# A short-convolution mixer: the planner's order of VectorE, ScalarE, GpSimd and SyncE replaced by a table

## The chip, the cores and the metric

The kernel runs on one core of one Trainium2 chip. The metric is the time of one execution in microseconds of the device. Before the change the median of three runs is 757.72 us (756.49 to 759.22).

## The reference

The model has one layer, a gated short convolution between two RMS norms; everything is float32, 1024 positions by 1024 features.

```python
u = rms_norm(x, pre_norm)                      # (1024, 1024)
z, bg, cg, v = split(u @ w_in, 4, axis=-1)     # w_in (1024, 8192), four of 2048
y = bg * causal_dwconv(cg * v, conv_w) * silu(z)   # three taps along the positions
m = y @ w_out                                  # w_out (2048, 1024)
out = x + rms_norm(m, post_norm)
```

## The kernel before, in words

**The matrix products.** TensorE multiplies fp32r. To keep float32 accuracy each operand is split into a high half (rounded to fp32r) and a low half (the rest), and each product is three matmuls: low by high, high by low, high by high. Both matrix products are computed in 2x2 blocks with seven products, called a, b, c, e, d, f, g, in place of eight. The weights of a product are then a block or a sum of blocks. For b, f and g a second level of the same kind lies inside, with 256 wide products; its weights have names that begin with d.

**The names.** A name in the profile is that of the tile:

- raw is a 256 KB block of w_in that SyncE's queue has loaded; se, sc and sf are sums of blocks, dsb, dsf and dsg those of the second level. They are made by GpSimd (`add_s`, L791; `deep_sums`, L1439).
- wah, wch, weh, wdh and dwb1h, dwf1h and so on are high halves, copied by ScalarE; wal, wcl, wel, wdl, dwb1l, dwf1l, dwf2l are the low halves, subtracted by VectorE (`split`, L809; `split_low`, L840; `deep_prep`, L1454). For some of them ScalarE also copies the source into a PSUM bank, beside, from which VectorE reads (`split_by_bank`, L833).
- u_a to u_g are the stationary operands made of u. The place of u_g is lent out in the middle of the kernel, and `restore_u` (L1723) loads the source (ug) again and splits it, the low half on VectorE.
- px, pv, px2b, pv2b, py2b, px2f, pv2f are PSUM banks. Their contents are taken over into sna, snc and sne (ScalarE copies, VectorE adds), then cv holds the convolution on VectorE and s the gated result, which SyncE's queue stores.
- tb, t and t23 are sums of w_out for the second product. ry and ru are pages with its operands, oy and ou those operands split in halves (`split_pages`, L1620); po_x is its bank.
- acc holds a row tile of the result, xr the residual, gpost the post-norm's weights, ve_post the mean square and rs_post its inverse root, which GpSimd makes (`finish`, L1951).

**The loops.** The first product runs over chunks of 128 channels, two pairs of blocks for each (an even and an odd number, such as wcl_28 and wcl_29), with the second-level products between them; a new round of dwb, dwf and dwg comes with every chunk. From about 604 us the second product follows, in units a, c, e, d, g over four row tiles, with small ones between. Each engine runs its own instructions in the order in which they stand in its queue and waits at the head of it for what is missing.

**What sets the order.** The program writes its operations in the order of the algorithm, and from `plan.record()` (L1780) to `plan.flush(PLAN)` (L2107) they are only recorded: 6577 operations, 4038 of them matmuls, 940 for VectorE, 392 for GpSimd, 794 for ScalarE and 412 for SyncE. `call` (L290) notes what each needs, `link` (L354) ties them, `deadlines` (L375) works out from modelled durations when each has to be done for TensorE not to wait, with a table that shifts the due times of single operations (`PLAN["boost"]`). `arrange` (L428) then runs a model of the engines in time: the due operation next for each engine, one lock between VectorE and GpSimd, and a free page out of 32 for each tile (`home`, L645). Where VectorE has nothing to do it takes an addition from GpSimd (`take`). TensorE's order is that of the program throughout. `emit` (L658) issues what came out. Since all recorded operations are issued from one line, they all have L292 in the profile before. The start of the kernel, to about 48 us, and the work behind the last matmuls (`finish_last`) are issued without a plan.

Of the kernel before, what the change touches and what calls it, by code (L numbers as in the profile page):

```python
# [27 lines left out]
PLAN = {  # L28
    "end": 14.0,
    "psum": 3.0,  # L30
    "store": 6.0,
    "turns": 1,
    "apart": 11.0,
    "hard": 2.0,
    "lock": 0.3,
    "sum": 10.0,
    "early": 0.0,
    "gap": 0.5,
    "least": 1.0,
    "free": 40.0,  # L40
    "take": 11.0,
    "held": {"snc_1": 1.95},
    "ahead": {"sync": 24.0, "gpsimd": 18.0, "scalar": 11.0, "vector": 11.0},
    "busy": {"vector": 1.9, "scalar": 0.3, "gpsimd": -2.1},
    "slack": {"tensor": 1.0, "gpsimd": 0.8, "sync": 1.0, "scalar": 0.1, "vector": 0.1},
    "boost": {
# [38 lines left out]
    },  # L85
}
# [123 lines left out]
U_SLOTS = (5, 4, 2, 6, 1, 3, 0, 0, 5, 2, 6, 4, 1, 3, 0, 5, 2, 6, 4, 1, 6, 3, 0, 4, 2, 5, 6, 1, 0, 3, 2, 4, 5, 6, 0, 4, 1, 5, 3, 6, 0, 2)  # L210
# [8 lines left out]
class Shelves:  # L219

    def __init__(self, ctx, tc):
        self.at, self.slots = {}, list(U_SLOTS)
        for n, (slots, room) in enumerate(U_LAYOUT):
            pool = ctx.enter_context(tc.tile_pool(name=f"up{n}", bufs=1))
            self.at.update({s: pool for s in slots})
            if n == 0:
                self.low = ctx.enter_context(tc.tile_pool(name="low_pages", bufs=1))
            gap(ctx, tc, f"room{n}", room)

    def tile(self, shape, dtype, tag, **kw):  # L230
        s = self.slots.pop(0)
        return self.at[s].tile(shape, dtype, tag=f"u{s}", **dict(kw, bufs=1))
# [21 lines left out]
class Plan:  # L254
# [120 lines left out]
    def deadlines(self, p):  # L375

        ops = self.ops
        limit = {}
        for op in ops:
            op.est = 0.0  # L380
        for turn in range(p["turns"]):
            for op in reversed(ops):
                if op.engine == "tensor":
                    op.late = op.ideal
                    continue
                late = op.pos + p["end"]
                for o in op.feeds:
                    f = ops[o]
                    late = min(late, f.late - op.lat - (p["hard"] if f.engine == "tensor" else 0.0) - (p["lock"] if op.lock else 0.0))
                for t in op.tiles:  # L390
                    if t in limit and all(x.key != t.key for x in op.news):
                        late = min(late, limit[t] - op.lat)
                if any(t.summed for t in op.tiles):
                    late = min(late, max(op.ideal, op.est) + p["psum"])
                if op.engine == "sync" and any(isinstance(a, View) and a.tile.space == "sbuf" for a in op.args[1:]):
                    late = min(late, max(op.ideal, op.est) + p["store"])
                if op.tiles and not op.news and all(t.space == "dram" for t in op.tiles):
                    late = min(late, max(op.ideal, op.pos) + p["sum"])
                op.late = late
            for op in ops:  # L400
                if op.engine != "tensor":
                    op.late = max([ops[o].late + 0.01 for o in op.needs], default=op.late) if op.needs and max(ops[o].late for o in op.needs) >= op.late else op.late
                op.est = max([ops[o].est + ops[o].lat for o in op.needs] + [op.late - p["ahead"].get(op.engine, 10.0) if op.news else 0.0, 0.0])
                if op.engine == "tensor":
                    op.est = op.ideal
# [22 lines left out]
    def arrange(self, p):  # L428
# [4 lines left out]
        for n, by in p.get("boost", {}).items():  # L433
            ops[n].late -= by
# [1699 lines left out]
```

## Time and profile before

| what | value |
|---|---|
| median of 3 runs | 757.72 us (756.49 to 759.22) |
| profiled execution, its own time | 758.85 us |
| its span in the trace | 757.1 us |
| granted TensorE clock | 0.998 |
| idle PE between 300 and 740 us | 2.69 us |
| waits of weight loads, 300 to 750 us | 6.1 us in 11 |

PE is TensorE's matmuls, PEld its weight loads, DVE is VectorE, ACT ScalarE, POOL GpSimd and SP SyncE. The matmuls are pipelined, so their ends are modelled, and the spans of GpSimd are rough. A row of a timeline has start, length, engine, line, operation and the output and inputs by the names above, without their numbers. In square brackets stands the idle time of the engine just before, with what ended it. In a view of waits a row names who waited, what for, the sum in us, how many times and the longest.

### The profile page before, as it was taken

To read this page: it belongs to the slowest core of one execution; us is meant where nothing else is said; L and a number is where in the kernel's file an instruction comes from. 1 tells how busy PE (TensorE), PEld (TensorE's weight loads), DVE (VectorE), ACT (ScalarE), POOL (GpSimd) and SP (SyncE) were. 2 spreads that over 40 slices of the span, in tenths; PEclk is the share of its full clock that TensorE was granted. 3 is DMA by queue.
4 is the path that set the end of the run, shared out by engine and by line. 5 is a ranking of instruction groups with operands and counts; after the bars stand their busy time and mean duration, and the time that the engine had idled before them with its cause. 6 is when DMAs were issued, how large, how long until landed. Compare 5 with 4: busy or idle time off the path is not lost.

```text
span 757.1 us, 12810 instructions
## 1 busy us (share of the span) xinstructions
PE 745.2 (98%) x4320; PEld 660.0 (87%) x4320; DVE 677.9 (90%) x1022; ACT 458.7 (61%) x880; POOL 462.4 (61%) x416
## 2 busy tenths in 40 slices
PE   8999999999999999999999999999999999999996
PEld 7888889999999999989998988899888889889885
DVE  6899988999998988999999999898999999877994
ACT  7765588675656564655556565666553666565831
POOL 2509997889686777697788777685739100600421
PEclk9999999999999999999999999999999999999999
DMA  9313325244333548476949383928465999566842
GB/s 313 78 49 91 111 77 162 102 142 133 98 119 98 177 115 224 111 193 163 264 119 273 95 239 80 270 95 217 118 183 179 339 362 309 201 226 206 283 149 111
DMA packets 117137, 130.11 MB, mean 172 GB/s; under 512 B 7320, under 2 KB 74704, under 8 KB 116944
## 3 DMA queue, kind: packets, MB, share of 16 engines
q1 hardware_dynamic: 112560, 120.77, 50.1%
q0 software_dynamic: 4352, 8.39, 7.2%
q8 instruction: 34, 0.56, 0.3%
q14 instruction: 31, 0.25, 0.1%
q10 hardware_dynamic: 160, 0.14, 0.1%
HBM read 101.74 MB, written 44.30 MB: 193 GB/s over the span
## 4 chain that ended last, share of the span: by engine, by line
PE 75%; DVE 8%; POOL 6%; issue 4%; DMA 3%; ACT 3%; SPq 0%; POOLq 0%; DVEq 0%; ACTq 0%
PE px L292 29%; PE pv L292 12%; PE po_x L292 8%; PE px2b L292 4%; PE po_v L292 3%; PE pp L292 3%; PE px2f L292 3%; PE px2g L292 2%; PE pv2f L292 2%; PE pv2b L292 2%; PE pb_x L292 1%; POOL dsb L292 1%; DMA raw<-in_sc_w_in 1%; PE py L292 1%; PE py2b L292 1%
## 5 line engine op out<-in xcount | busy, mean ns | idle before, releaser
L292 PE MATMUL px<-u_a,wah 128*128 128x512 f32 x248 | 75.1, 383 | 0.0
L292 PE MATMUL px<-u_c,wch 128*128 128x512 f32 x248 | 74.9, 382 | 0.0
L292 PE MATMUL px<-u_d,wdh 128*128 128x512 f32 x248 | 74.9, 382 | 0.0
L292 PE MATMUL pv<-u_e,weh 128*128 128x512 f32 x248 | 74.7, 381 | 0.0
L292 ACT COPY beside<-raw 128x512 f32<-128x512 f32 x67 | 39.6, 591 | 34.2 <-DVE dwf2l L292 9.9
L292 PEld LDWEIGHTS px<-u_a,wah 128*128 128x128 f32 x248 | 46.5, 188 | 8.0
L292 PEld LDWEIGHTS px<-u_c,wch 128*128 128x128 f32 x248 | 46.5, 188 | 7.9
L292 PEld LDWEIGHTS pv<-u_e,weh 128*128 128x128 f32 x248 | 46.5, 188 | 7.7
L292 PEld LDWEIGHTS px<-u_d,wdh 128*128 128x128 f32 x248 | 46.5, 188 | 7.6
L292 DVE SCALAR_TENSOR_TENSOR cv<-gpad,cw,cv 128x1024 f32<-128x1024 f32 x32 | 49.8, 1557 | 3.3 <-ACT cv L292 3.2
L292 POOL TENSOR_TENSOR sf<-raw,sc 128x512 f32<-128x512 f32 x30 | 44.5, 1484 | 7.1 <-DVE sc L292 5.5
L292 PE MATMUL px<-u_c,wcl 128*128 128x512 f32 x124 | 47.9, 386 | 0.2 <-DVE wcl L292 0.2
L292 PE MATMUL px<-u_a,wal 128*128 128x512 f32 x124 | 47.8, 385 | 0.0
L292 PE MATMUL px<-u_d,wdl 128*128 128x512 f32 x124 | 47.7, 385 | 0.0
L292 PE MATMUL pv<-u_e,wel 128*128 128x512 f32 x124 | 47.5, 383 | 0.0
L292 POOL TENSOR_TENSOR sc<-se,raw 128x512 f32<-128x512 f32 x25 | 35.9, 1434 | 19.0 <-DVE se L292 10.4
L292 POOL TENSOR_TENSOR rs_post<-ve_post,minus_half 128x1 f32<-128x1 f32 x7 | 6.5, 941 | 65.9 <-DVE ve_post L292 65.9
L292 POOL TENSOR_TENSOR raw<-raw,raw 128x512 f32<-128x512 f32 x31 | 43.5, 1403 | 4.2 <-DVE se L292 3.8
L292 POOL TENSOR_TENSOR se<-raw,raw 128x512 f32<-128x512 f32 x22 | 32.2, 1463 | 18.7 <-DMA raw<-in_sc_w_in 9.4
L292 ACT COPY sna<-px 128x512 f32<-128x512 f32 x30 | 17.6, 585 | 34.4 <-PE px L292 34.4
L292 DVE TENSOR_TENSOR wcl<-sc,wch 128x512 fp32r<-128x512 f32 x31 | 33.8, 1089 | 5.0 <-ACT wch L292 5.0
L292 DVE TENSOR_TENSOR wel<-se,weh 128x512 fp32r<-128x512 f32 x31 | 32.3, 1043 | 0.0
(486 smaller groups left out, 2615.8 us busy)
## 6 DMA issues: line engine op xcount, KB each, us to landing
raw<-in_sc_w_in SPq DMA_DIRECT2D x128, 256.0 KB, 5.2
y_d<-cv SPq DMA_DIRECT2D x16, 512.0 KB, 2.7
s_d<-s SPq DMA_DIRECT2D x32, 256.0 KB, 4.9
t_d<-in_sc_w_out POOLq DMA_DIRECT2D x16, 512.0 KB, 8.5
tb<-in_sc_w_out SPq DMA_DIRECT2D x16, 256.0 KB, 3.5
t_d<-in_sc_w_out SPq DMA_DIRECT2D x16, 256.0 KB, 4.9
t_d<-t_d SPq DMA_DIRECT2D x16, 256.0 KB, 4.6
s<-y_d SPq DMA_DIRECT2D x16, 256.0 KB, 4.6
```

What stands on the lines that cost most here:

```text
L292: getattr(engine, name)(*(self.plain(a) for a in args), **{k: self.plain(a) for k, a in kw.items()})
```

## The change

The planner goes, with its costs, its shifted due times and its choice of pages. In its place stand three tables. `ORDER` lists the operations by their number, and a negative number stands for so many matmuls; `HOMES` gives the page of each tile as it comes up; `BY_VECTOR` names 48 additions that the program writes for GpSimd and that VectorE makes. `arrange` only reads the tables. `U_SLOTS`, the places of the u operands, is looked up by name and no longer by turn.

```diff
-PLAN = {
-    "end": 14.0,
-    "psum": 3.0,
...
-    "boost": {
-        0: -1.88, 1: 31.37, 2: -1.93, 4: 16.59, 5: 18.27, 6: 0.14, 20: 0.84, 21: 1.2, 22: 10.67, 27: -0.09,
...
-}
+ORDER = (
+    350, 0, 1, -4, 5, 60, -2, 203, 22, -3, 2, -3, 6, 20, 21, -2, 24, -3, 246, -3, 7, 4, 25, 41, -2, 3, 247, -2, 23, -5, 42, -1, 91,
...
+)
+
+HOMES = (
+    15, 16, 21, 22, 24, 29, 31, 19, 20, 1, 15, 27, 16, 14, 18, 26, 12, 2, 22, 20, 21, 16, 3, 24, 26, 27, 1, 31, 17, 19, 30, 23, 22,
...
+)
+
+BY_VECTOR = (
...
+    2671, 2672, 2674, 2810, 2867, 2868, 3028, 3147, 3399, 3593, 3948, 4110, 4248, 4464, 4605, 4606, 4662, 4840, 5780, 5782, 5783,
+    6354, 6363, 6432, 6445,
+)
...
-U_SLOTS = (5, 4, 2, 6, 1, 3, 0, 0, 5, 2, 6, 4, 1, 3, 0, 5, 2, 6, 4, 1, 6, 3, 0, 4, 2, 5, 6, 1, 0, 3, 2, 4, 5, 6, 0, 4, 1, 5, 3, 6, 0, 2)
+U_SLOTS = {
+    "u_a": 5, "u_b": 4, "u_c": 2, "u_e": 6, "u_d": 1, "u_f": 3, "xb": 0, "u_g": 0, "ou_a0": 5, "oy_a0": 2,
...
-        s = self.slots.pop(0)
+        s = U_SLOTS[kw["name"]]
...
-    def deadlines(self, p):
...
-    def flush(self, p):
         self.link()
-        order = self.arrange(p)
-        self.emit(order)
-
-    def arrange(self, p):
...
+        self.emit(self.arrange())
+
+    def arrange(self):
+
+        ops, order, homes = self.ops, [], iter(HOMES)
+        matmuls = iter([op for op in ops if op.engine == "tensor"])
+        for n in ORDER:
+            order += [next(matmuls) for _ in range(-n)] if n < 0 else [ops[n]]
+        for n in BY_VECTOR:
+            ops[n].engine, ops[n].name = "vector", (self.nc.vector, ops[n].name[1])
+        for op in order:
+            for x in sorted(op.news, key=lambda x: x.n):
+                if x.key[1] == "pg":
+                    x.slot = next(homes)
+        self.slots = list(homes)
+        assert len(order) == len(ops)
         return order
...
-    def home(x, slots):
...
-            plan.flush(PLAN)
+            plan.flush()
```

What is computed, the matmuls, their order and the operations themselves stay. VectorE gets 954 of the recorded operations (940 before), GpSimd 378 (392 before): net, 17 additions go from GpSimd to VectorE (thirteen before the last stage; four are acc<-acc,xr of the last stage) and 3 from VectorE to GpSimd. Up to about 48 us, and behind the last matmul, each engine's order is the same as before. The recorded operations now have L449. The number at the end of a name in the rows below counts tiles, and it is not the same number before and after; the number ahead of it is that of the block, the chunk or the row tile.

**The first place: VectorE at about 543 to 550 us**, where u_g is restored and wcl_29 made. cv is the convolution, s0 and s4 the gated sums, sna, sne and snc what was taken over from the banks. Before:

```order
L292 TENSOR_TENSOR cv_13_6384<-cv_13_6384,sna_27_6067 128x512
L292 TENSOR_TENSOR sne_28_6426<-px_28_6278,sne_28_6426 128x512
L292 SCALAR_TENSOR_TENSOR s0_13_6365<-s1_13_6276,s0_13_6365 128x512
L292 TENSOR_TENSOR u_g_584<-ug_6346,u_g_584 128x2x256
L292 SCALAR_TENSOR_TENSOR s4_13_6522<-cv_13_6384,s0_13_6365 128x512
L292 TENSOR_TENSOR snc_28_6396<-px2f_14_6461,snc_28_6396 128x256
L292 TENSOR_TENSOR wcl_29_6537<-sc_29_6391,wch_29_6441 128x512
```

After:

```order
L449 TENSOR_TENSOR u_g_584<-ug_6294,u_g_584 128x2x256
L449 TENSOR_TENSOR sne_28_6438<-px_28_6289,sne_28_6438 128x512
L449 TENSOR_TENSOR cv_13_6392<-cv_13_6392,sna_27_6066 128x512
L449 SCALAR_TENSOR_TENSOR s0_13_6300<-s1_13_6262,s0_13_6300 128x512
L449 TENSOR_TENSOR wcl_29_6511<-sc_29_6397,wch_29_6446 128x512
L449 SCALAR_TENSOR_TENSOR s4_13_6534<-cv_13_6392,s0_13_6300 128x512
L449 TENSOR_TENSOR snc_28_6402<-px2f_14_6463,snc_28_6402 128x256
```

u_g went ahead of the cv product with sna_27, of sne_28 and of s0_13; wcl_29 went ahead of s4_13 and snc_28.

**The second place: VectorE and GpSimd at about 325 to 331 us**, where dwf1l_8 (a low half of the second level) and its source dsf0_8 are made. VectorE before:

```order
L292 TENSOR_TENSOR sne_16_3784<-px_16_3640,sne_16_3784 128x512
L292 TENSOR_TENSOR snc_16_3751<-px2f_8_3814,snc_16_3751 128x256
L292 TENSOR_TENSOR wel_17_3872<-se_17_3714,weh_17_3826 128x512
L292 TENSOR_TENSOR snc_16_3751<-pv_16_3748,snc_16_3751 128x512
L292 TENSOR_TENSOR sna_16_3671<-px2b_8_3774,sna_16_3671 128x256
L292 TENSOR_TENSOR sna_17_3867<-pv2b_8_3875,sna_17_3867 128x256
L292 TENSOR_TENSOR dwf1l_8_3907<-dsf0_8_3816,dwf1h_8_3898 128x512
```

VectorE after:

```order
L449 TENSOR_TENSOR sne_16_3775<-px_16_3643,sne_16_3775 128x512
L449 TENSOR_TENSOR dwf1l_8_3875<-dsf0_8_3810,dwf1h_8_3834 128x512
L449 TENSOR_TENSOR sna_16_3670<-px2b_8_3772,sna_16_3670 128x256
L449 TENSOR_TENSOR snc_16_3756<-px2f_8_3825,snc_16_3756 128x256
L449 TENSOR_TENSOR snc_16_3756<-pv_16_3750,snc_16_3756 128x512
L449 TENSOR_TENSOR sna_17_3863<-pv2b_8_3880,sna_17_3863 128x256
L449 TENSOR_TENSOR wel_17_3914<-se_17_3707,weh_17_3865 128x512
```

dwf1l_8 went ahead of the step of sna_16, both of snc_16, that of sna_17 and of wel_17; wel_17 went from the third place to the last. GpSimd before, from the first half of dsf0_8 to its second:

```order
L292 TENSOR_TENSOR t23_13_3808<-tb1_13_3703,tb0_13_3697 128x256
L292 TENSOR_TENSOR dsf0_8_3816<-sf_17_3755 128x256
L292 TENSOR_TENSOR t23_13_3808<-t23_13_3808,tb0_13_3697 128x256
L292 TENSOR_TENSOR tb1_13_3703<-tb1_13_3703,t23_13_3808 128x256
L292 TENSOR_TENSOR dsb1_8_3852<-raw_16_01_3459,raw_17_01_3664 128x256
L292 TENSOR_TENSOR dsb1_8_3852<-raw_16_01_3459,dsb0_8_3745 128x256
L292 TENSOR_TENSOR dsf0_8_3816<-dsf0_8_3816,sf_16_3668 128x256
```

GpSimd after:

```order
L449 TENSOR_TENSOR dsf0_8_3810<-sf_17_3767 128x256
L449 TENSOR_TENSOR t23_13_3808<-t23_13_3808,tb0_13_3648 128x256
L449 TENSOR_TENSOR dsf0_8_3810<-dsf0_8_3810,sf_16_3650 128x256
L449 TENSOR_TENSOR tb1_13_3806<-tb1_13_3806,t23_13_3808 128x256
L449 TENSOR_TENSOR dsb1_8_3856<-raw_16_01_3454,raw_17_01_3613 128x256
L449 TENSOR_TENSOR dsb1_8_3856<-raw_16_01_3454,dsb0_8_3736 128x256
```

The second half of dsf0_8 went ahead of the tb1 step and of both halves of dsb1_8, and the first t23_13 step isn't GpSimd's any more.

**The third place: the last stage, about 710 to 724 us.** GpSimd before, the inverse roots and the additions of the residual:

```order
L292 TENSOR_TENSOR rs_post0_8335<-ve_post0_8328,minus_half_90 128x1
L292 TENSOR_TENSOR rs_post1_8337<-ve_post1_8330,minus_half_90 128x1
L292 TENSOR_TENSOR acc_7302<-acc_7302,xr01_7923 128x512
L292 TENSOR_TENSOR acc_7302<-acc_7302,xr11_8033 128x512
L292 TENSOR_TENSOR rs_post2_8411<-ve_post2_8388,minus_half_90 128x1
L292 TENSOR_TENSOR rs_post3_8413<-ve_post3_8391,minus_half_90 128x1
L292 TENSOR_TENSOR acc_7302<-acc_7302,xr21_8254 128x512
L292 TENSOR_TENSOR acc_7302<-acc_7302,xr31_8274 128x512
```

VectorE after, the same additions among the steps on acc and the splits of oy_d and ou_g:

```order
L449 SCALAR_TENSOR_TENSOR acc_7385<-acc_7385,rs_post0_8320,gpost1_7233 128x512
L449 TENSOR_SCALAR ve_post1_8352<-so_7664 128x1
L449 SCALAR_TENSOR_TENSOR acc_7385<-acc_7385,rs_post0_8320,xr00_8018 128x512
L449 TENSOR_TENSOR acc_7385<-acc_7385,xr01_7734 128x512
L449 SCALAR_TENSOR_TENSOR acc_7385<-acc_7385,rs_post1_8359,xr10_8016 128x512
L449 TENSOR_TENSOR oy_d1_8247<-ry_d13_8096,oy_d1_8247 128x512
L449 TENSOR_SCALAR ve_post3_8386<-so_7664 128x1
L449 SCALAR_TENSOR_TENSOR acc_7385<-acc_7385,rs_post1_8359,gpost1_7233 128x512
L449 TENSOR_TENSOR acc_7385<-acc_7385,xr11_8020 128x512
L449 TENSOR_TENSOR ou_g0_8344<-ru_g01_8213,ou_g0_8344 128x512
```

The additions of xr01 and xr11 stand on VectorE between the scaled steps on acc; those of xr21 and xr31 follow further down, and GpSimd keeps the roots alone.

More of the change, by code (lines that the diff above doesn't have):

```diff
@@ L1 @@
-import heapq
 from contextlib import ExitStack
@@ L27 @@
 )
-PLAN = {
-    "end": 14.0,
-    "psum": 3.0,
[L31 to L45, printed above, removed]
-    "boost": {
[38 rows of a table removed]
-    },
-}
+ORDER = (
[164 rows of a table added]
+)
+HOMES = (
[35 rows of a table added]
+)
+BY_VECTOR = (
+    1, 201, 249, 286, 333, 351, 353, 745, 895, 1012, 1039, 1096, 1390, 1391, 1448, 1451, 1598, 1743, 1800, 1807, 1958, 2153, 2307,
+    2671, 2672, 2674, 2810, 2867, 2868, 3028, 3147, 3399, 3593, 3948, 4110, 4248, 4464, 4605, 4606, 4662, 4840, 5780, 5782, 5783,
+    6354, 6363, 6432, 6445,
+)
 BY_BANK_DEEP = (("b", 0), ("b", 1), ("b", 2), ("f", 0), ("f", 2))
@@ L209 @@
 LOW_PAGES = (3, 10, 11, 13, 15, 16, 5, 6, 8, 9)
-U_SLOTS = (5, 4, 2, 6, 1, 3, 0, 0, 5, 2, 6, 4, 1, 3, 0, 5, 2, 6, 4, 1, 6, 3, 0, 4, 2, 5, 6, 1, 0, 3, 2, 4, 5, 6, 0, 4, 1, 5, 3, 6, 0, 2)
+U_SLOTS = {
+    "u_a": 5, "u_b": 4, "u_c": 2, "u_e": 6, "u_d": 1, "u_f": 3, "xb": 0, "u_g": 0, "ou_a0": 5, "oy_a0": 2,
[4 rows of a table added]
+}
 def gap(ctx, tc, name, size):
@@ L221, in __init__ @@
     def __init__(self, ctx, tc):
-        self.at, self.slots = {}, list(U_SLOTS)
+        self.at = {}
         for n, (slots, room) in enumerate(U_LAYOUT):
@@ L373, in link @@
                 self.users.setdefault(t, []).append(op)
-    def deadlines(self, p):
[L377 to L405, printed above, removed]
-            allocs, tiles = {}, {}
-            for op in ops:
-                for t in op.news:
-                    allocs.setdefault(t.key, []).append(op.late)
-            for t, users in self.users.items():
-                if t.space != "dram":
-                    tiles.setdefault(t.key, []).append((max(u.est + u.lat for u in users), t.n, t))
-            for key, ts in tiles.items():
-                at = sorted(allocs.get(key, []))
-                spare = self.spare(key)
-                for k, (end, _, t) in enumerate(sorted(ts, key=lambda x: x[:2])):
-                    if k + spare < len(at):
-                        limit[t] = max(at[k + spare] - p["gap"], end + p["least"])
@@ L644, in home, with flush @@
-    @staticmethod
-    def home(x, slots):
-        name = x.kw["name"]
-        low, high = ([s for s in slots if (s in LOW_PAGES) == side] for side in (True, False))
-        if name[:2] in ("wb", "wf", "wg"):
-            first = low
-        elif name[0] == "w" or name[:2] == "dw":
-            first = high
-        else:
-            first = slots
-        s = (first or slots)[0]
-        slots.remove(s)
-        return s
+    def flush(self):
+        self.link()
+        self.emit(self.arrange())
```

203 lines of the change are left out of this document (removed), and 238 rows, old and new, of tables (HOMES, ORDER, PLAN, U_SLOTS).

## The prediction

> **What bounds the kernel now.** The measure of "no change" is 0.3%, some 2.3 us. The profiled execution took 758.85 us: a span of 757.1 us and 1.75 us around it. It lies 1.13 us above the median of 757.72, so the sum is made against 758.85, and 1.13 is taken off at the end. I read the page's busy line first.
>
> ```profile
> PE 745.2 (98%) x4320; PEld 660.0 (87%) x4320; DVE 677.9 (90%) x1022; ACT 458.7 (61%) x880; POOL 462.4 (61%) x416
> ```
>
> TensorE comes first, VectorE follows at 90%. Whether that is one regime or several is told by the table of stretches. The columns are start and end, length, and then busy time (with instructions) of PE, PEld, DVE, ACT and POOL, granted clock, DMA share and GB/s.
>
> ```profile
> 48.00:300.00 252.00, 252.00 (x1468) 224.88 (x1468) 230.91 (x337) 163.54 (x322) 203.55 (x181) 1.00 0.42 124
> 300.00:340.00 40.00, 39.61 (x246) 35.56 (x245) 36.68 (x56) 22.95 (x45) 30.74 (x28) 1.00 0.63 161
> 340.00:440.00 100.00, 99.27 (x610) 89.01 (x609) 93.81 (x137) 58.54 (x112) 78.86 (x72) 1.00 0.70 188
> 440.00:560.00 120.00, 118.49 (x731) 106.35 (x730) 111.37 (x172) 72.24 (x139) 78.59 (x72) 1.00 0.65 172
> 560.00:740.00 180.00, 179.94 (x993) 157.35 (x992) 161.56 (x251) 103.29 (x200) 53.27 (x41) 1.00 0.72 242
> ```
>
> The clock is full throughout, and the order of the matmuls isn't touched, so all that a new order of the other engines can win is time in which TensorE stands still. From 48 to 300 us there is none. From 300 to 740 PE is idle for 0.39+0.73+1.51+0.06 = 2.69 us. VectorE has 252-230.91, 3.32, 6.19, 8.63 and 18.44 us free in the five, 57.67 in all: it isn't full, it is late at certain places. Since matmuls are pipelined, I took the places not from PE but from the waits of its weight loads, 300 to 750 us. The columns are what waited, for whom, us in all, times, the longest.
>
> ```profile
> PEld px2b L292 <- DVE dwb1l L292: 2.0, 3, 1.1
> PEld px L292 <- DVE u_g L292: 1.4, 1, 1.4
> PEld px2f L292 <- DVE dwf1l L292: 0.8, 1, 0.8
> PEld px L292 <- ACT dwb L292: 0.6, 1, 0.6
> PEld po_x L292 <- DVE ou_g L292: 0.4, 1, 0.4
> PEld pv2f L292 <- DVE dwf2l L292: 0.3, 1, 0.3
> PEld px L292 <- ACT sna L292: 0.2, 1, 0.2
> PEld po_x L292 <- issue: 0.2, 1, 0.2
> PEld px L292 <- DVE wdl L292: 0.2, 1, 0.2
> ```
>
> That is 11 waits and 6.1 us, nearly all for low halves that VectorE makes (a name ending in l, u_g and ou_g): **6.1 us is the whole prize**, or 2.69 if PE's own idle time counted. I take 6.1, for a weight load that waits holds the matmul behind it. The Trainium skill's page "Perfetto Trace Analysis", section "Identifying the Most-Contended Engine", says the same from its side: matmul busy time is a poor measure of how near a kernel is to its limit, since pipelined instructions look smaller, and the busy time of the weight loads is the better one. [...]
>
> **Part 1: the two late pieces at 542 to 550 us.** VectorE's timeline (start, length, engine, operation, out<-in):
>
> ```profile
> 543.62 1.22 DVE L292 TENSOR_TENSOR cv<-cv,sna 128x512 f32<-128x512 f32 x1
> 544.77 0.68 DVE L292 TENSOR_TENSOR sne<-px,sne 128x512 f32<-128x512 f32 x1
> 545.37 0.68 DVE L292 SCALAR_TENSOR_TENSOR s<-s,s 128x512 f32<-128x512 f32 x1
> 545.97 1.21 DVE L292 TENSOR_TENSOR u_g<-ug,u_g 128x512 fp32r<-128x512 f32 x1
> 547.10 1.99 DVE L292 SCALAR_TENSOR_TENSOR s<-cv,s 128x512 f32<-128x512 f32 x1
> 549.01 0.41 DVE L292 TENSOR_TENSOR snc<-px2f,snc 128x256 f32<-128x256 f32 x1
> 549.34 0.68 DVE L292 TENSOR_TENSOR wcl<-sc,wch 128x512 fp32r<-128x512 f32 x1
> ```
>
> VectorE works without a break here: the 1.4 us wait is a matter of place in the row. The new order puts u_g ahead of sne, of the product cv<-cv,sna and of s, and so starts it 545.97-543.62 = 2.35 us earlier. That is more than 1.4: the wait goes. It puts wcl ahead of the second s and of snc, another 549.34-547.10 = 2.24 us. To wcl I also give the 0.6 us that the view puts down to a ScalarE copy (dwb): the low half ends at 550.02, when that wait ends. Removed: 2.0 us. What is next late is what was pushed back: sne, s and cv feed no matmul directly, they empty banks and make the stored sums.
>
> **Part 2: the deep weights.** These are the halves of the second level, made in every round of chunks. At 327 to 331 us:
>
> ```profile
> 326.85 0.41 DVE L292 TENSOR_TENSOR snc<-px2f,snc 128x256 f32<-128x256 f32 x1
> ...
> 329.02 0.41 DVE L292 TENSOR_TENSOR sna<-pv2b,sna 128x256 f32<-128x256 f32 x1
> 330.13 1.11 DVE L292 TENSOR_TENSOR dwf1l<-dsf,dwf1h 128x512 fp32r<-128x512 f32 x1 [0.71 <-ACT dwf1h L292]
> ```
>
> Here VectorE's row isn't all: dwf1l also waited 0.71 us for ScalarE's high half, which waits for GpSimd's sum dsf. So moving dwf1l forward on VectorE alone would only lengthen that idle time. GpSimd's row:
>
> ```profile
> 325.74 1.18 POOL L292 TENSOR_TENSOR tb<-tb,t 128x256 f32<-128x256 f32 x1
> ...
> 328.72 0.73 POOL L292 TENSOR_TENSOR dsf<-dsf,sf 128x256 f32<-128x256 f32 x1
> ```
>
> The new order puts tb and the two that make dsb (left out here) behind dsf, which so starts 328.72-325.74 = 2.98 us earlier, and on VectorE the five between 326.85 and 329.43 behind dwf1l, 2.6 us. Both are more than 0.8: the wait goes. Next late is wel, now behind dwf1l and four others; in the old order it stood ahead of them, so its lead shrinks by about dwf1l and three short ones, some 2 us.
>
> For dwb1l, the 2.0 us are three rounds, 1.1, 0.4 and 0.5; the middle one is
>
> ```profile
> PEld px2b L292 <- DVE dwb1l L292: 0.4, 1, 0.4
> ```
>
> In the first (its low half at 398.8 us), the row ahead of it is
>
> ```profile
> 396.54 0.41 DVE L292 TENSOR_TENSOR sna<-py2b,sna 128x256 f32<-128x256 f32 x1
> 396.87 0.89 DVE L292 TENSOR_TENSOR s<-cv,s 128x512 f32<-128x512 f32 x1
> 397.68 1.22 DVE L292 TENSOR_TENSOR wcl<-sc,wch 128x512 fp32r<-128x512 f32 x1
> ```
>
> and the first two now stand behind dwb1l: 397.68-396.54 = 1.14 us against 1.1, just enough. In the middle round an sne and an s go behind it, by the rows above 0.60 us each from start to start, 1.2 against 0.4. In the third its neighbours stay: 0.5 to 0.6 remains. wdl (0.2) is ahead of a 128x256 subtraction that stood before it (0.33 us, as sna above): it goes. dwf2l (0.3) and sna (0.2) aren't clearly changed: they stay. Removed in this part: 0.8+1.1+0.4+0.2 = 2.5 us.
>
> **Part 3: the additions that change engine.** Net, 17 move from GpSimd to VectorE and 3 the other way. Thirteen of the 17 lie before the last stage; at 0.6 to 1.2 us each (sne and cv above) they are 8 to 16 us, minus the three, inside 57.67 us of free VectorE time. I cost them at nothing; the cover is that idle time, and where it is gone locally it shows as a new wait, costed below. Four are the additions acc<-acc,xr of the last stage:
>
> ```profile
> L292 POOL TENSOR_TENSOR acc<-acc,xr 128x512 f32<-128x512 f32 x4 | 6.9, 1734 | 1.3 <-DVE acc L292 1.3
> 711.13 0.75 DVE L292 SCALAR_TENSOR_TENSOR acc<-acc,rs_post,xr 128x512 f32<-128x512 f32 x1
> 711.80 1.78 DVE L292 SCALAR_TENSOR_TENSOR acc<-acc,rs_post,gpost 128x512 f32<-128x512 f32 x1
> ...
> 715.86 0.68 DVE L292 TENSOR_TENSOR ou_d<-ru_d,ou_d 128x512 fp32r<-128x512 f32 x1
> ```
>
> While GpSimd adds, VectorE's instruction with two inputs in SBUF takes 1.78 us in place of 0.75. So each addition already costs VectorE 1.03 us, 4.1 for four. Moved over, they cost 0.60 to 0.68 us each (ou_d's row), 2.4 to 2.7, so VectorE comes out about 1.5 us earlier, against 0.4 us for ou_g and 0.2 of issue behind it: 0.6 goes. If no time came back, VectorE would be 2.7 us later at the same place; I take the first, since the two acc rows are the same form 0.67 us apart. The Trainium skill's page "Perfetto Trace Analysis", section "Optimizing Scalar/DVE Operations", speaks against taking work onto a full VectorE: it would rather have work go to ScalarE or GpSimd, yet warns that GpSimd and VectorE share a read port, so that moving between them may not help. By its first half these four cost 2.7 us, by its second they return what GpSimd held; the 1.78 beside 0.75 is this trace's agreement with the second.
>
> **Part 4: pages and loads.** The tiles' pages are dealt anew, and a load waits until its page is free. A weight load is 256 KB:
>
> ```profile
> raw<-in_sc_w_in SPq DMA_DIRECT2D x128, 256.0 KB, 5.2
> ```
>
> No weight load of PE waits for a DMA in the rows above, so the loads' lead is more than zero; how much, the trace doesn't say. Bounds: nothing, or a few loads a little late, up to 1.5 us (a quarter of the 6.1 us). Below nothing it can't go, as no wait for a load stands there to be removed. I take nothing, as that row is the nearest.
>
> **Sum.** Removed: 2.0+2.5+0.6 = 5.1 us. Staying: 1.0. An order that gives some pieces lead takes it from others (wel, the later pieces of the last stage); I allow two or three new waits of today's mean, 6.1/11 = 0.55: 1.4 us. Net 3.7: 758.85-3.7 = 755.15, and less 1.13 it is **754.0**.
>
> **The rivals.** *The same:* in the last stage no port time comes back. Then ou_g's 0.6 stays, VectorE is 2.7 us later, and of the 5.1 there remain 5.1-0.6-2.7-1.4 = 0.4 us: 757.3. For it speaks that VectorE is 90% busy there too (161.56 of 180); against it the 1.78 beside 0.75. *Slower:* head-of-line blocking. A low half that stands early in VectorE's queue holds all behind it while it waits for its high half; dwf1l does so already, 0.71 us at 330 us, and it comes 13 times:
>
> ```profile
> L292 DVE TENSOR_TENSOR dwf1l<-dsf,dwf1h 128x512 fp32r<-128x512 f32 x13 | 11.7, 896 | 2.4 <-ACT dwf1h L292 2.3
> ```
>
> If GpSimd's sum doesn't keep pace and each round waits 0.7 us and TensorE with it, that is 9.1 us against 5.1-0.8 = 4.3: 4.8 slower, 762.5. It decides from (4.3+2.3)/13 = 0.51 us a round. For it: the row shows 2.3 us of such waiting already. Against it: GpSimd's dsf moves forward with it at the place looked at, and 0.7 us on VectorE reaches TensorE only where no lead is left. *All goes:* none of the waits is left and no new one comes, 758.85-6.1-1.13 = 751.6. For it: most leads gained (2.35, 2.24, 2.6) are well over the waits; against it: the third dwb1l is unchanged. That the change does nothing can't be: the rows of three engines differ.
>
> **How the numbers follow.** The forecast 0.53, everything gone 0.15, the same 0.22, slower 0.10. Faster by over 0.3% (below 755.45) are the first two: 0.68. The range holds the first three: up from 751.2 (751.6, and the rounding of 11 waits to 0.1 us) to 757.6 (757.3, and a little of part 4).
>
> **What would show it.** Right: in the waits of PE's loads u_g, dwf1l and the dwb1l at 398 us are missing, their sum is near 2.4 us, PE's busy time per stretch fills up by what went, VectorE's rows in the last stage have no 1.78 beside the additions, and there is one dwb1l left near 472 us. Wrong: new weight-load waits of over 2 us in all (wel, dwf1l, raw), VectorE idle for a ScalarE high half in most rounds, a PE that is slower per matmul at the same waits, or a span that shortens by 2.7 us or less though the load waits are gone, which would say that PE's idle time was the prize.

## The result, and the profile after

The changed kernel takes 753.94 us, median of five runs (753.37 to 754.67). The kernel before took 758.89 us, the median of five runs (756.49 to 759.32), among them the three of before. The ratio is 0.9942, with an interval of 0.9925 to 0.9960: 3.0 to 5.7 us faster. The forecast was 754.0. The profiled execution took 754.67 us, with a span of 752.9, which is 4.2 us shorter than the span before (757.1); 3.7 was forecast.

First the weight loads' waits, the view from which the forecast was made, here from 48 to 752 us:

```profile
PEld px2g L449 <- ACT gs L449: 0.8, 1, 0.8
PEld px2b L449 <- DVE sna L449: 0.7, 1, 0.7
PEld px L449 <- ACT sna L449: 0.5, 1, 0.5
PEld px L449 <- issue: 0.2, 1, 0.2
```

Of the eleven old waits none is left, and four others have come, 2.2 us in all. The sum was forecast at 2.4, as 1.0 that stays and 1.4 that is new. The sum fits, its parts don't. The stretches (columns as before):

```profile
300.00:340.00 40.00, 39.75 (x248) 35.78 (x246) 34.12 (x54) 23.26 (x45) 33.69 (x29) 1.00 0.68 181
340.00:440.00 100.00, 99.11 (x611) 89.45 (x612) 87.46 (x143) 58.47 (x112) 74.56 (x69) 1.00 0.67 185
440.00:560.00 120.00, 120.00 (x749) 109.06 (x748) 110.44 (x177) 73.59 (x142) 82.02 (x74) 1.00 0.65 173
```

PE's idle time from 300 to 560 us went from 2.63 to 0.25+0.89 = 1.14 us, 1.5 us less, for a span that is 4.2 shorter: PE's own idle time wasn't the prize, the loads' waits were (3.9 less). VectorE's busy time fell, from 36.68 to 34.12 and from 93.81 to 87.46 us in the first two, though in the second it does more instructions (143, 137 before). Over the span it went from 677.9 to 662.4, with 14 instructions more. That was in no term of the sum.

The place of u_g, on VectorE:

```profile
539.93 0.84 DVE L449 TENSOR_TENSOR u_g<-ug,u_g 128x512 fp32r<-128x512 f32 x1
540.70 0.68 DVE L449 TENSOR_TENSOR sne<-px,sne 128x512 f32<-128x512 f32 x1
541.30 0.68 DVE L449 TENSOR_TENSOR cv<-cv,sna 128x512 f32<-128x512 f32 x1
541.90 1.22 DVE L449 SCALAR_TENSOR_TENSOR s<-s,s 128x512 f32<-128x512 f32 x1
543.05 1.22 DVE L449 TENSOR_TENSOR wcl<-sc,wch 128x512 fp32r<-128x512 f32 x1
```

u_g and wcl stand where the order put them, and no load waits there. In the last stage the three kinds of step on acc (instances, then shortest, median and longest in ns):

```profile
L449 DVE SCALAR_TENSOR_TENSOR acc<-acc,rs_post,gpost x4: 743/748/751, 706.0 to 714.0; 128x512 f32<-128x512 f32 x4
L449 DVE SCALAR_TENSOR_TENSOR acc<-acc,rs_post,xr x4: 743/749/751, 706.8 to 720.4; 128x512 f32<-128x512 f32 x4
L449 DVE TENSOR_TENSOR acc<-acc,xr x4: 685/686/691, 707.5 to 718.5; 128x512 f32<-128x512 f32 x4
```

No step takes 1.78 us any more. Of the signs that the prediction named for "right", the missing waits, their sum (2.2 for 2.4) and the last stage are there. Two are not: no dwb1l waits near 472 us any more, and PE's idle time from 340 to 440 us did not fill up, it went from 0.73 to 0.89. Of the signs for "wrong" one is there by its size: the new waits are 2.2 us in all, over the 2 that it named, but not at wel, dwf1l or raw. The experiments asked whether these places are where the time came from.

### The profile page after: what moved, and what is told of

Read it like the earlier page. It is cut to its first block, busy times and chain, and to the rows that moved or that the text cites. A ratio compares the mean times of both kernels' runs of the same rounds, so it can differ in the third digit from the quotient of the medians.

```text
span 752.9 us, 12726 instructions
## 1 busy us (share of the span) xinstructions
PE 742.5 (99%) x4320; PEld 660.1 (88%) x4320; DVE 662.4 (88%) x1036; ACT 456.1 (61%) x880; POOL 443.3 (59%) x402
## 4 chain that ended last, share of the span: by engine, by line
PE 93%; DMA 2%; DVE 1%; POOL 1%; issue 1%; ACT 1%; POOLq 0%; DVEq 0%; ACTq 0%
PE px L449 38%; PE pv L449 14%; PE po_x L449 11%; PE px2b L449 5%; PE px2f L449 3%; PE px2g L449 3%; PE pp L449 3%; PE po_v L449 3%; PE pv2b L449 2%; PE pv2f L449 2%; DMA raw<-in_sc_w_in 2%; PE pb_x L449 1%; PE pf_x L449 1%; PE py2b L449 1%; PE py L449 1%; PE pv2g L449 1%
## 5 line engine op out<-in xcount | busy, mean ns | idle before, releaser
L449 PE MATMUL px<-u_a,wah 128*128 128x512 f32 x248 | 75.2, 383 | 0.0
L449 PE MATMUL px<-u_d,wdh 128*128 128x512 f32 x248 | 74.9, 382 | 0.0
L449 PE MATMUL px<-u_c,wch 128*128 128x512 f32 x248 | 74.6, 381 | 0.0
L449 PE MATMUL pv<-u_e,weh 128*128 128x512 f32 x248 | 74.5, 381 | 0.0
L449 ACT COPY beside<-raw 128x512 f32<-128x512 f32 x67 | 39.5, 590 | 25.8 <-DVE wal L449 10.0
L449 PEld LDWEIGHTS px<-u_a,wah 128*128 128x128 f32 x248 | 46.5, 188 | 8.1
L449 PEld LDWEIGHTS px<-u_c,wch 128*128 128x128 f32 x248 | 46.5, 188 | 7.7
L449 PEld LDWEIGHTS px<-u_d,wdh 128*128 128x128 f32 x248 | 46.5, 188 | 7.6
L449 POOL TENSOR_TENSOR sf<-raw,sc 128x512 f32<-128x512 f32 x30 | 46.4, 1548 | 11.4 <-DVE sc L449 2.7
L449 PEld LDWEIGHTS pv<-u_e,weh 128*128 128x128 f32 x248 | 46.5, 188 | 7.5
L449 POOL TENSOR_TENSOR raw<-raw,raw 128x512 f32<-128x512 f32 x31 | 46.3, 1494 | 10.9 <-DVE se L449 10.4
L449 ACT COPY sna<-px 128x512 f32<-128x512 f32 x30 | 17.6, 586 | 57.2 <-PE px L449 41.9
L449 DVE SCALAR_TENSOR_TENSOR cv<-gpad,cw,cv 128x1024 f32<-128x1024 f32 x32 | 45.8, 1433 | 3.5 <-ACT cv L449 3.2
L449 POOL TENSOR_TENSOR rs_post<-ve_post,minus_half 128x1 f32<-128x1 f32 x7 | 6.0, 851 | 71.6 <-DVE ve_post L449 71.6
L449 PE MATMUL px<-u_c,wcl 128*128 128x512 f32 x124 | 47.6, 384 | 0.3 <-ACT sna L449 0.3
L449 PE MATMUL px<-u_a,wal 128*128 128x512 f32 x124 | 47.8, 385 | 0.0
L449 PE MATMUL px<-u_d,wdl 128*128 128x512 f32 x124 | 47.6, 384 | 0.0
L449 PE MATMUL pv<-u_e,wel 128*128 128x512 f32 x124 | 47.3, 382 | 0.0
L449 POOL TENSOR_TENSOR sc<-se,raw 128x512 f32<-128x512 f32 x22 | 31.0, 1410 | 21.1 <-issue 8.1
L449 POOL TENSOR_TENSOR se<-raw,raw 128x512 f32<-128x512 f32 x20 | 29.2, 1461 | 12.8 <-DMA raw<-in_sc_w_in 9.1
L449 DVE TENSOR_TENSOR wcl<-sc,wch 128x512 fp32r<-128x512 f32 x31 | 28.5, 921 | 5.5 <-ACT wch L449 5.1
L449 POOL TENSOR_TENSOR cv<-cv,sne 128x512 f32<-128x512 f32 x13 | 18.7, 1439 | 22.1 <-DVE cv L449 22.1
```

The lines of the kernel that those rows point to most:

```text
L449: getattr(engine, name)(*(self.plain(a) for a in args), **{k: self.plain(a) for k, a in kw.items()})
```

## The experiments

The three tables can be written for the kernel before as well: with its own order, pages and engines in them, each engine's instructions come out as in the kernel before. Single operations were then moved in one table or the other. The kernel before ran beside each group; its medians there are 758.25 (35 runs), 758.26 (23) and 758.06 us (35). The first group (b_u, b_tail, b_deep, b_vec) ran on another chip than the other two, so ratios are what is compared between groups.

### One place at a time, on the kernel before

**u_g and wcl alone (b_u).** VectorE's queue:

```diff
+TENSOR_TENSOR u_g<-ug,u_g
 TENSOR_TENSOR cv<-cv,sna
 TENSOR_TENSOR sne<-px,sne
 SCALAR_TENSOR_TENSOR s0<-s1,s0
-TENSOR_TENSOR u_g<-ug,u_g
+TENSOR_TENSOR wcl<-sc,wch
 SCALAR_TENSOR_TENSOR s4<-cv,s0
 TENSOR_TENSOR snc<-px2f,snc
-TENSOR_TENSOR wcl<-sc,wch
```

> The kernel before with two moves on VectorE alone: u_g goes ahead of the cv product, sne and s (543 to 546 us), wcl goes ahead of the next s and of snc (547 to 549 us). If a weight load's wait is time lost for good (place in the row), the waits of 1.4 and 0.6 us are missing from the waits of PE's loads, no other comes in their place, and the span is 2.0 us shorter: 756.9 against 758.9 us. If TensorE only comes earlier to its next wait (absorbed), the sum of the waits stays near 6 us and the time within 0.5 us of before.

Measured: 758.26 us, 12 runs, ratio 1.0004 (0.9993 to 1.0014): nothing won. On VectorE and then on PE, by their timelines:

```profile
545.16 1.22 DVE L467 TENSOR_TENSOR u_g<-ug,u_g 128x512 fp32r<-128x512 f32 x1
546.30 1.22 DVE L467 TENSOR_TENSOR cv<-cv,sna 128x512 f32<-128x512 f32 x1
547.44 0.68 DVE L467 TENSOR_TENSOR sne<-px,sne 128x512 f32<-128x512 f32 x1
```

```profile
548.26 0.46 PE L467 MATMUL px<-u_g,wgl 128*128 128x512 f32 x1 [0.64 <-DVE sne L467]
```

The wait for u_g is gone, and TensorE waits for sne instead: sne empties the bank px, into which the product with u_g goes. My edit had left sne behind the cv product, which the changed kernel does not. So it was tried again.

**The same place, in exactly the order of the changed kernel (b_u2):** u_g, sne, cv, s0, wcl, s4, snc.

```diff
+TENSOR_TENSOR u_g<-ug,u_g
+TENSOR_TENSOR sne<-px,sne
 TENSOR_TENSOR cv<-cv,sna
-TENSOR_TENSOR sne<-px,sne
 SCALAR_TENSOR_TENSOR s0<-s1,s0
-TENSOR_TENSOR u_g<-ug,u_g
+TENSOR_TENSOR wcl<-sc,wch
 SCALAR_TENSOR_TENSOR s4<-cv,s0
 TENSOR_TENSOR snc<-px2f,snc
-TENSOR_TENSOR wcl<-sc,wch
```

> The kernel before with u_g, sne, the cv product, s, wcl, s, snc in exactly the order of the changed kernel (the first try had left sne behind the cv product, and TensorE then waited 0.8 us for the bank that sne empties). If the place is worth its waits where the bank is cared for, the 1.4 and 0.6 us go and nothing takes over: 756.3 against 758.3 us. If VectorE is simply behind in that stretch and passes the wait on, the time stays within 0.7 us of before, and new waits stand after 550 us.

Measured: 757.67 us, 12 runs (755.65 to 760.30), ratio 0.9998 (0.9986 to 1.0010): at most 1.1 us of the 2.0 can be there. The waits of the weight loads in its profile:

```profile
PEld px2b L467 <- DVE dwb1l L467: 1.5, 1, 1.5
PEld px L467 <- ACT dwf2h L467: 0.9, 1, 0.9
PEld pv2f L467 <- DVE dwf2l L467: 0.4, 1, 0.4
PEld px L467 <- DVE wdl L467: 0.2, 1, 0.2
```

u_g's wait is gone. The 0.9 us put down to dwf2h is the product with wcl, at 546.5 us. wcl was early in the row, but took

```profile
545.28 1.99 DVE L467 TENSOR_TENSOR wcl<-sc,wch 128x512 fp32r<-128x512 f32 x1
```

since GpSimd added dsf and issued a transfer beside it. Two rounds of dwb1l and the 0.8 us of dwf1l are missing here too, and nothing was done to them: with the same instructions up to 541 us, such waits change from one execution to the next, which fits the kernel before's own times of 755.92 to 760.42 us.

**dwf1l with its chain (b_deep), and on VectorE alone (b_vec).**

```diff
 b_deep, GpSimd          dsf0_8<-dsf0_8,sf    ahead of tb1_13 and both halves of dsb1_8
 b_deep, ScalarE         dwf1h_8<-dsf0_8      ahead of three copies
 b_deep and b_vec, VectorE
+TENSOR_TENSOR dwf1l_8<-dsf0_8,dwf1h_8
 TENSOR_TENSOR snc_16<-px2f_8,snc_16
 TENSOR_TENSOR wel_17<-se_17,weh_17
 TENSOR_TENSOR snc_16<-pv_16,snc_16
 TENSOR_TENSOR sna_16<-px2b_8,sna_16
 TENSOR_TENSOR sna_17<-pv2b_8,sna_17
-TENSOR_TENSOR dwf1l_8<-dsf0_8,dwf1h_8
```

> The kernel before with one chain of the second level moved forward, near 328 us: on GpSimd the second half of dsf ahead of tb and both halves of dsb, on ScalarE dwf1h ahead of three copies, on VectorE dwf1l ahead of five steps. If place in the row on all three engines is what counts, the 0.8 us wait for dwf1l goes, VectorE's 0.71 us idle ahead of dwf1l goes, and the span is 0.8 us shorter: 758.1 us. If the late pieces behind it (dwb2l, wel) take over, a wait of 0.3 to 1 us stands at them, and the time stays.

> As the run before, but on VectorE alone: dwf1l ahead of the same five steps, GpSimd and ScalarE as they were. If the head of a queue blocks what is behind it, dwf1l starts no earlier than its high half allows, VectorE idles about 3.3 us (0.71 and the 2.6 of the five steps) in place of 0.71, dwf1l's wait of 0.8 us stays, and the five steps are 2 to 3 us later, wel still with lead (its matmul comes 4.6 us after it before): 758.9 us or up to 1 us more. If VectorE's own row is what counts, the 0.8 us go: 758.1 us.

Measured: b_deep 758.52 us, 11 runs, ratio 1.0003 (0.9988 to 1.0018); b_vec 760.17 us, 11 runs, ratio 1.0022 (1.0007 to 1.0037). On VectorE alone the move makes the kernel slower, by 0.5 to 2.8 us. VectorE in b_vec:

```profile
325.62 0.68 DVE L467 TENSOR_TENSOR sne<-px,sne 128x512 f32<-128x512 f32 x1
329.06 1.10 DVE L467 TENSOR_TENSOR dwf1l<-dsf,dwf1h 128x512 fp32r<-128x512 f32 x1 [2.77 <-ACT dwf1h L467]
330.09 0.41 DVE L467 TENSOR_TENSOR snc<-px2f,snc 128x256 f32<-128x256 f32 x1
```

The head of the queue blocked it for 2.77 us (3.3 was expected), and the loads there wait 0.4 us for dwf2l and 0.3 us for snc, which stand behind. With the chain moved along (b_deep), dwf1l starts some 3 us earlier, VectorE's idle time ahead of it is 0.68 us (0.71 before; it was to go), and its own wait is missing. But that wait is missing in other profiles of this order as well, so the run can't tell what the move is worth, and the time doesn't show it.

**The four additions of the last stage (b_tail):** only their engine was changed.

> The kernel before with the four additions acc<-acc,xr of the last stage on VectorE in place of GpSimd, at their old place in the program. If the port time comes back, the rows of 1.77 to 1.78 us beside them fall to 0.75 or less, VectorE is about 1.5 us earlier at the last splits, and the waits for ou_g and issue (0.6 us) go: 758.3 us. If nothing comes back, VectorE is 2.7 us later there, the wait for ou_g grows from 0.4 to up to 3.1 us: 759 to 761.6 us.

Measured: 758.26 us, 12 runs, ratio 1.0002 (0.9991 to 1.0013). In its profile all steps on acc take 0.75 us or less and the waits for ou_g and issue are missing: the port time came back, as forecast. The 0.6 us don't show in the median, but they lie inside the interval (0.9991 is 0.7 us).

### Engines or order

**The engines of the one with the order and the pages of the other (b_eng, a_eng).** One line of the table differs from the kernel before and the changed kernel:

```diff
 b_eng: ORDER and HOMES of the kernel before
+BY_VECTOR of the changed kernel (48)
 a_eng: ORDER and HOMES of the changed kernel
+BY_VECTOR of the kernel before (34)
```

> The kernel before, its order and pages, with only the engines of the changed kernel: the same 17 operations go to VectorE and 3 to GpSimd, each at its old place in the program. The run that took away u_g's wait alone won nothing, so the order at a place is not the whole cause. If the engines are (GpSimd's hold on VectorE's instructions with two SBUF inputs), VectorE's busy time falls by 10 us or more from 677.9 and the time goes to 754 to 755.5 us. If the order or the pages are, the time stays at 758 to 758.5.

> The changed kernel, its order and pages, with the engines of the kernel before (the 17 back on GpSimd, the 3 on VectorE). If the engines are the cause, 757.5 to 758.5 us, and VectorE's busy time goes from 662.4 back toward 677. If the order or the pages are, 753.5 to 755, and VectorE's busy time stays below 668.

Measured: b_eng 757.67 us, 12 runs, ratio 0.9986 (0.9973 to 0.9999), VectorE busy 676.7 us. a_eng 753.25 us, 6 runs (753.02 to 754.37), ratio 0.9936 (0.9921 to 0.9951), VectorE busy 663.0. So the engines are worth some 1 us on the old order (2.0 at most by the interval) and nothing that can be seen on the new one. Order and pages together bring the gain and also VectorE's shorter busy time. a_eng's profile has no wait of a weight load after 48 us at all, with a span of 751.2 us. Its time and that of the changed kernel (0.9942) can't be told apart.

### The changed kernel with places undone

**u_g and wcl back (a_u), and all named places back (a_undo):** dwf1l with its chain, dwb1l near 397 and 434 us, wdl, u_g, wcl, and the four additions on GpSimd.

```diff
 a_u and a_undo, VectorE
-TENSOR_TENSOR u_g<-ug,u_g
-TENSOR_TENSOR sne<-px,sne
 TENSOR_TENSOR cv<-cv,sna
+TENSOR_TENSOR sne<-px,sne
 SCALAR_TENSOR_TENSOR s0<-s1,s0
-TENSOR_TENSOR wcl<-sc,wch
+TENSOR_TENSOR u_g<-ug,u_g
 SCALAR_TENSOR_TENSOR s4<-cv,s0
 TENSOR_TENSOR snc<-px2f,snc
+TENSOR_TENSOR wcl<-sc,wch
...
```

> The changed kernel with this one place undone: on VectorE the cv product, sne, s, u_g, s, snc, wcl as before. If the place carries its own part of the gain, u_g and wcl let PE wait again, 1 to 2 us: 755 to 756 us. If the changed order has VectorE far enough ahead there, no wait or one under 0.5 us: 754 us.

> The changed kernel with all the named places undone together: u_g and wcl near 540 us, dwf1l with its chain on GpSimd and ScalarE near 326 us, dwb1l near 397 and 434 us, wdl near 410 us, and the four additions of the last stage back on GpSimd. If these places make up the gain, most of the 5.1 us come back: 757.5 to 759 us. If the gain lies in the lead of all pieces, under 2.5 us come back: 754 to 756.4 us.

Measured: a_u 754.66 us, 12 runs, ratio 0.9956 (0.9942 to 0.9970); a_undo 754.57 us, 12 runs, ratio 0.9958 (0.9944 to 0.9973). Against 753.94 all the places together are worth some 0.6 us, and by the two intervals at most some 3, not 5.1. In a_undo's profile dwf1l (0.8) and dwb1l (1.0) do wait again; u_g, wcl, wdl and ou_g don't: VectorE gets there early enough even in the old row. In a_u's profile u_g doesn't wait either, but the product with wcl does, 0.8 us at 547 us.

### The loads and the pages

**A store behind the loads (a_sp).** The new waits at 417 to 420 us come from a load. On GpSimd after the change:

```profile
414.29 1.28 POOL L449 TENSOR_TENSOR se<-raw,raw 128x512 f32<-128x512 f32 x1 [6.83 <-DMA raw<-in_sc_w_in]
```

```diff
 SyncE's queue
-DMA s_d<-s4_9
 DMA tx_d<-tb1_15
 DMA raw_22<-in_sc_w_in (four)
+DMA s_d<-s4_9
```

> The changed kernel with one store of s on SyncE's queue moved behind the four loads of the next pair's weights, near 403 us. There the queue waits 3.7 us for VectorE's s with the loads behind it, GpSimd then idles 6.8 us for a load, ScalarE's high halves are late, and a copy behind them lets PE wait 0.8 and 0.5 us at 417 to 420 us. If that chain is right, the loads start about 3.5 us earlier, GpSimd's idle time halves, and both waits go: 752.6 us. If the pages or the sums hold the loads anyway, 754 us and the waits stay.

Measured: 754.07 us, 6 runs (752.99 to 754.49), ratio 0.9942 (0.9927 to 0.9957). GpSimd's idle time for that load is gone, and so are the two waits at 417 and 420 us:

```profile
PEld px2b L452 <- DVE sna L452: 0.6, 1, 0.6
PEld px L452 <- DVE wdl L452: 0.3, 1, 0.3
PEld px L452 <- issue: 0.2, 1, 0.2
```

The span is 1.1 us shorter in this one execution, but the median is the same. The chain was right; its price, some 1.3 us, doesn't show in the time.

**The same order and engines on other pages (a_pages, a_pages2).** Only `HOMES` differs, in 964 of 1152 entries.

```diff
 a_pages:  each tile takes the page whose last use lies furthest back in the program
 a_pages2: each tile takes the page that came free earliest in the trace of the changed kernel
-HOMES of the changed kernel
+HOMES dealt anew
```

> The changed kernel with its order and engines, but 964 of 1152 tiles on other pages: each takes the page that has been free longest, by the rule of the kernel before (weights of b, f and g on the lower pages, the other weights on the upper). If the pages are part of the cause, the time rises by 1 us or more, with DMAs or copies that wait for a page. If they are not, 753.5 to 754.5 us.

> The changed kernel with pages dealt anew once more, 964 of 1152, but each tile takes the page that came free earliest by the times of the changed kernel's own trace, so that few wait for one (the first new deal took them in the order of the program, and VectorE, ScalarE and GpSimd then waited for pages that a store or a load still held). If only such waits made that deal slow, 753.5 to 754.5 us. If it matters which page it is, it stays at 757 us or more.

Measured: a_pages 758.92 us, 12 runs, ratio 1.0011 (0.9997 to 1.0025); a_pages2 758.25 us, 12 runs (756.30 to 761.45), ratio 1.0011 (0.9995 to 1.0027). **Either deal takes the whole gain away, with no instruction moved on any engine.** In a_pages some engines wait for pages, VectorE for one that a store still held:

```profile
DVE dwb2l L452 <- DMA s_d<-s: 3.5, 1, 3.5
```

In a_pages2 VectorE waits for no transfer. Its load waits:

```profile
PEld px L452 <- issue: 3.1, 2, 2.9
PEld px L452 <- ACT snc L452: 1.0, 1, 1.0
PEld px2b L452 <- DVE sna L452: 0.7, 1, 0.7
PEld po_x L452 <- ACT jk L452: 0.3, 1, 0.3
```

The 2.9 us lie at 383 us, at the product with wcl. VectorE there, and GpSimd beside it:

```profile
379.11 1.37 DVE L452 TENSOR_TENSOR sne<-snc,sne 128x512 f32<-128x512 f32 x1
380.41 5.62 DVE L452 TENSOR_TENSOR wcl<-sc,wch 128x512 fp32r<-128x512 f32 x1
385.95 0.68 DVE L452 TENSOR_TENSOR wel<-se,weh 128x512 fp32r<-128x512 f32 x1
```

```profile
379.87 1.16 POOL L452 DMA_DIRECT2D t_d<-in_sc_w_out  x1
380.63 1.73 POOL L452 TENSOR_TENSOR se<-raw,raw 128x512 f32<-128x512 f32 x1
381.88 1.16 POOL L452 TENSOR_TENSOR tb<-tb 128x256 f32<-128x256 f32 x1
382.58 1.68 POOL L452 TENSOR_TENSOR raw<-raw,raw 128x512 f32<-128x512 f32 x1
383.81 1.66 POOL L452 TENSOR_TENSOR sc<-se,raw 128x512 f32<-128x512 f32 x1
```

One subtraction of 0.68 us stands for 5.62 us, until four instructions of GpSimd in a row have ended (385.47). The same place in the changed kernel:

```profile
380.73 0.68 DVE L449 TENSOR_TENSOR wcl<-sc,wch 128x512 fp32r<-128x512 f32 x1
```

```profile
380.20 1.15 POOL L449 DMA_DIRECT2D t_d<-in_sc_w_out  x1
381.56 1.61 POOL L449 TENSOR_TENSOR se<-raw,raw 128x512 f32<-128x512 f32 x1 [0.22 <-issue]
```

Here GpSimd's addition starts 0.83 us after VectorE's subtraction, which is through by then (381.41), and VectorE isn't held. On the new pages it starts 0.22 us after it by the (rough) records, and VectorE loses. That is no chance shift in time: up to there the two executions differ by 0.3 us, and VectorE's subtraction starts equally far behind GpSimd's transfer in both (0.53 and 0.54 us). The tables show what differs. In the changed kernel `HOMES` gives this se page 8, on which sc lies until VectorE's wcl has read it: GpSimd can't begin before wcl is done, and its start at 381.56 agrees (the view names nobody for the 0.22 us of idle time). In a_pages2 the same se gets page 18, in a_pages page 2, both used last by TensorE, and GpSimd runs on. In a_pages VectorE is held at the same place, one subtraction later:

```profile
382.97 4.43 DVE L452 TENSOR_TENSOR wel<-se,weh 128x512 fp32r<-128x512 f32 x1
```

So the pages here set an order between two engines that the program doesn't ask for. In the profiled executions a_pages2's span is 3.4 us longer than the changed kernel's (756.3 against 752.9), and 2.9 us is the wait behind this one subtraction. Whether it comes in every execution isn't recorded.

## Why the prediction was right, and where its working was not

**The prize: right.** 6.1 us of load waits, not PE's 2.69 of idle time. In all fourteen profiled kernels the span less the sum of these waits is 750.5 to 752.3 us: before 757.1-6.1 = 751.0, changed 752.9-2.2 = 750.7, a_eng 751.2-0. So a load's wait costs its length, as closely as this range of 1.8 us tells, and with none left (a_eng) the span is 751.2. The busy time of the weight loads doesn't show the gain, 660.0 us before and 660.1 after; their waits do.

**The net sum: right in size.** 3.7 us against 4.2 in the profiled executions, 754.0 against 753.94. That rests on how much of the 6.1 would go, not on which. That the two times agree to 0.1 us is luck: 6.1 us of waits went and 2.2 came where 5.1 and 1.4 were priced, undoing the priced places brought back some 0.6 (a_undo), and the kernel before itself came out 1.2 us above the median from which the forecast started (758.89 and 757.72).

**Part 1 (2.0 us): failed as a term.** "What is next late: sne, s and cv feed no matmul directly" broke in b_u: they empty banks, and TensorE waited for an emptied bank as for a weight (0.64 us for sne). In the order of the changed kernel sne stands early and that wait doesn't come, but wcl took 1.99 us beside GpSimd where the row before had 0.68, and its product waited 0.9 us (b_u2). The place alone won no more than 1.1 us there, and undoing it cost 0.7 us, within the uncertainty (a_u). u_g's wait is no accident of one profile: it is in all four others of that order in which u_g wasn't moved, with 0.9 to 1.4 us.

**Part 2 (2.5 us): failed as a term.** That VectorE's move alone would only lengthen its idle time was right (b_vec), and so was that the chain starts earlier when all three engines move (b_deep). But the 0.8 us for dwf1l is in none of the four other profiles of that order in which dwf1l wasn't moved (b_u, b_u2, b_tail, b_eng), and dwb1l waits in three rounds in two of the six, in one round in four. I priced a single profile's waits as if each came every time.

**Part 3: the engines at nothing was nearly right** (b_eng 0.14%, at most 0.27; a_eng not distinguishable). The port time returned as said (1.78 to 0.75), worth at most 0.7 us in the time.

**Part 4 (pages at nothing, bound 1.5 us): wrong.** The deal of pages is worth 4.3 to 5.0 us (758.25 and 758.92 against 753.94): with a different one the same order is as slow as the kernel before. I looked for loads that wait for a page and found none. That a page also decides for which engine GpSimd's next sum has to wait, and with that whether it runs beside VectorE's subtraction, was not in the working.

**The rivals.** The head of a blocked queue is real (b_vec). In the changed kernel VectorE's idle time for dwf1h even grew, from 2.3 to 6.2 us over the 13 rounds, 0.48 a round where the prediction let it decide from 0.51, but no load waited for dwf1l. As in "all goes", none of the eleven old waits is left, but four new ones came.

**What makes the difference**, as far as the runs show it: order and pages together, not the named places and not the engines. The old order on other pages was not run, so what the order brings by itself is not shown. VectorE's instructions run shorter in the changed kernel. The group of 31 wcl subtractions (shortest, median and longest in ns) before, after, and in a_pages2:

```profile
L292 DVE TENSOR_TENSOR wcl<-sc,wch x31: 673/1208/1775, 41.4 to 583.6; 128x512 fp32r<-128x512 f32 x31
```

```profile
L449 DVE TENSOR_TENSOR wcl<-sc,wch x31: 674/693/1667, 41.4 to 579.9; 128x512 fp32r<-128x512 f32 x31
```

```profile
L452 DVE TENSOR_TENSOR wcl<-sc,wch x31: 674/1041/5618, 40.9 to 583.6; 128x512 fp32r<-128x512 f32 x31
```

Over 0.85 us there are 21 of the 31 before, 14 after and 18 in a_pages2, each with a GpSimd instruction beside it. Counted in the timelines, VectorE has 9 instructions over 2.05 us before and 7 or 8 in the six other kernels with its order and pages; it has 2 in the changed one and 2 to 4 in the four others with its order and pages, and 4 and 5 on the new pages. This goes along with the times only loosely: a_eng, among the fastest, has 4 as well, and VectorE's busy time is still 667.6 and 670.2 us on the new pages, where the whole gain is gone. How long a hold is and where it falls says more than how many there are, and the row of 5.62 us shows the mechanism at one place. That it carries the whole 5 us is not shown: no run here changes this one page alone, and for the other places it stays open what the pages do.

## What to carry to other kernels

Add up the waits of the busiest engine's weight loads to size a prize, but see from several executions which of them recur before one is priced. Where the time of a kernel varies by half a per cent from run to run, as here, a wait that is taken away alone need not show in the time. Test the part of a change that moves no instruction too (here the pages): on two other deals there was no gain. A page that is used again is also an order between engines, since the one that fills it waits for the one that still reads it. Where a piece moves forward in a queue, move its sources on the other engines with it, and count the steps that empty a bank as waited for.

## What the runs showed of the hardware

A VectorE subtraction with both inputs in SBUF can be held by several GpSimd instructions in a row: 5.62 us in place of 0.68, behind four of them (a_pages2), and 4.43 behind three (a_pages). The Trainium skill, page "SBUF — State Buffer", section "SBUF: two separate sides", says that VectorE with two SBUF inputs and a GpSimd instruction that reads SBUF share one port pair, which the first to start keeps for its whole instruction. The 1.78 beside 0.75 us agrees; the 5.62 goes beyond it, since VectorE's row lasts over four GpSimd instructions, and by the recorded starts, which are rough for GpSimd, VectorE had come first, by 0.22 us.

The times spread differently: 755.92 to 760.42 us for the kernel before in 35 runs, 753.37 to 754.67 for the changed one in five, 756.30 to 761.45 on other pages in twelve (a_pages2). But with places undone on the changed pages it is 752.99 to 757.36 in twelve (a_u), so that the narrow range belongs to the pages is not shown.
